# First two column blocks of a mixer's output projection multiplied together, three of eight ktile pairs by seven products of block sums

## The chip, the core and the metric

The kernel runs on one core of one Trainium2 chip. Its engines work side by side and in order: TensorE (in the profile PE, its weight loads PEld), VectorE (DVE), ScalarE (ACT), GpSimd (POOL) and SyncE (SP); SP and POOL also have queues from which transfers are issued. The time is the device time of one execution in microseconds; a run's value is compared as the median over executions, lower is better.

## What is computed

One layer of a decoder trunk on 256 tokens of width 2048. The part that matters is the mixer's end and what follows it:

```python
merged = g[:, :, 0] * (o_a @ w_o_mla) + g[:, :, 1] * (o_b @ w_o_swa)   # (256, 2048)
y = merged @ w_out                                                      # w_out: (2048, 2048)
x = x + rms_norm(y, norm_mix_post)
h = rms_norm(x, norm_ffn_pre)
x = x + rms_norm(conv_ffn(h, w_up, conv_w, conv_b, w_down), norm_ffn_post)
```

All arrays are float32.

## The kernel before

**Products.** A float32 operand is split into a high part that TensorE's fp32r form takes and the low rest. `mm3` (line 174) makes one product of three matmuls, high by high, high by low, low by high, each with a 128x128 block of activations as the stationary operand and 128x512 weights as the moving one. Weights come as raw tiles of 128x1024 float32 through a ring of three buffers (`raw_row`, `wchunk`; transfers on SP's queue). `convert` (line 134) makes the parts: a cast on ScalarE (line 143), the difference on VectorE (line 144). The results go into a ring of converted chunks, five deep in this part of the kernel (`RING` = 4 and one more from `flex[0] = "w"`, line 896). A chunk's buffer is free again when its matmuls are done.

**A projection.** `gemm` (line 179) makes one block of 512 output columns for both tiles of 128 tokens: 16 ktiles (128 rows of weights each), two ktiles a chunk, 16 x 2 x 3 = 96 matmuls into two PSUM banks. After each chunk it calls `tick`, which runs the work that `at` has put at that step; this is how work of one stage is written out between the matmuls of another. `drain` runs what is left. A scheduler then fixes each engine's order ahead of time; an engine doesn't change it at run time.

**The stages around the change.** `wo_a` is multiplied in four blocks (lines 835 to 843). After each, VectorE joins the two branches (lines 840 and 841), and in the next block's steps `m_cols` transposes the merged activations on TensorE and splits them (lines 820, 233, 234) into `mt`, eight tiles of two ktiles each. During the first of these blocks the gain `gpost` and the residual `x2` are loaded on SP's queue (`late_loads`, lines 804 to 810). Then `w_out` is multiplied in four blocks of 512 columns (lines 898 to 913). After each, `y_evac` squares it on ScalarE for the norm (line 857) and multiplies it by the gain on VectorE into `yg` (line 858). Block 3 finishes its first token tile ahead of the second; `resid` (line 865) then adds the normed result to `x2`, and the FFN begins.

**PSUM.** There are eight banks: four in `pacc`, two in `pss`, two in `pst`. All `gemm` calls of `wo_a` and `w_out` take two of `pacc`; the transposes of `m_cols` take `pst`.

**Seven products.** The FFN's down projection, later in the kernel, already has the other form. `down_pair` (line 1096) takes two column blocks and 12 ktile pairs. A ktile pair by two column blocks and two token tiles is a 2 by 2 product of blocks. A plain step (`p`) makes its eight block products, 24 matmuls. A seven step (`s`) makes seven, 21 matmuls, from sums of activation blocks (`token_sums`, line 1017, made once in an earlier stage) and differences of weight blocks (lines 1131 to 1134, on VectorE), with the Winograd form of Strassen's scheme. The results go to four banks `c` and four banks `q`; the latter are added together after the last seven (lines 1148 to 1152). The raw weights of a seven are loaded on POOL's queue (lines 1126, 1127). `PAIR_ORDER` (line 1240) gives the steps of the two pairs, `psppsppsppsp` and `ppsppsppsppp`.

Of the kernel before, what the change touches and what calls it, by code (L numbers as in the profile page):

```python
# [19 lines left out]
P = 128  # L20
D = 2048
# [20 lines left out]
def trunk_layer(ctx, tc, x, x_cols_in, conv_cols_in, g_mix_post, g_ffn_post, w_in, w_q, w_kv,  # L42
# [136 lines left out]
    def gemm(xh, xl, w, k0, nk, c0, n, split=None, extra=None, ps=None):  # L179
# [19 lines left out]
        return acc, todo  # L199

# [598 lines left out]
    x2_all = [sb(p3, [P, D], f"x2_{t}") for t in range(NT)]  # L799
    x2 = [[x_[:, j * 512:(j + 1) * 512] for j in range(4)] for x_ in x2_all]  # L800
    es6, p6 = open_pool("p6")
    gpost = sb(p6, [P, D], "gpost", tag="gp")
# [30 lines left out]
    for i in range(12):  # L833
        at(now[0] + 10 + 2 * i, lambda i=i: late_loads(i))
    for j in range(4):
        ld = merge_loads(j)
        acc, _ = gemm(AH, AL, wo_a, 0, KT, 512 * j, 512)
# [8 lines left out]
    yg_all = [[sb(p6, [P, 1024], f"yg_{t}_{j}", tag="f" + "ab"[t], bufs=2) for j in range(2)] for t in range(NT)]  # L846
    yg = [[yg_all[t][j // 2][:, (j % 2) * 512:(j % 2 + 1) * 512] for j in range(4)] for t in range(NT)]
# [6 lines left out]
    def y_evac(acc, b, t):  # L854
# [3 lines left out]
        vec.tensor_tensor(yg[t][j][:, o:o + n], acc[t][:, :n], gpost[:, c0:c0 + n], op=ALU.mult)  # L858
# [36 lines left out]

    flex[0] = "w"
    turn.update(raw=0, w=0)
    for b in range(4):
        c0, n = W_BLOCKS[b]
        last = b == 3  # L900
        acc, todo = gemm(MH_, ML_, w_out, 0, KT, c0, n, split=0 if last else None, extra={i: (px,) for i in range(EXTRA)} if last else None)
        if b == 0:
            drain()
            es4.close()
            es8, p8 = open_pool("p8")
# [111 lines left out]
    def token_sums(u):  # L1017
# [4 lines left out]
        g = gtiles[u].bitcast(F32)  # L1022
        a, m = (sb(s_pool[0], [P, 512], f"s{n}{u}", tag="hx", bufs=2) for n in "am")
        vec.tensor_tensor(a, g[:, 0:512], g[:, 512:1024], op=ALU.add)
        a11, a21, a12, _ = (a[:, i * P:(i + 1) * P] for i in range(4))
        m1, m2, m3, m4 = (m[:, i * P:(i + 1) * P] for i in range(4))
        vec.tensor_tensor(m1, a21, a[:, 384:512], op=ALU.add)
        vec.tensor_tensor(m3, a11, a21, op=ALU.subtract)
        vec.tensor_tensor(m2, m1, a11, op=ALU.subtract)
# [285 lines left out]
```

## Time and profile before

| | us |
|---|---|
| median of 3 runs (1471.06 to 1471.63) | 1471.11 |
| the profiled execution | 1471.75 |
| its span, from the first to the last instruction | 1470.0 |
| DVE busy in the span | 1023.2 |
| ACT busy in the span | 818.1 |

The page names each group of instructions by line of the kernel, engine, operation, and tile written and tiles read. "DVE wlo L144 <- ACT whi L143" in a list of waits says that VectorE's instruction of line 144 had to wait for ScalarE's of line 143; the numbers are total us, times and longest. Times within the execution count from the start of the span. In this count `wo_a`'s last block begins near 621 and `w_out` at 643.6; the down projection's two pairs run from 1004.5 to 1130.3. Some matmul records are missing from the trace.

### The profile page before, as it was taken

The numbers are of one execution on the slowest core, as the hardware profiler recorded it, in microseconds if no ns is written. First come the engines' busy times: TensorE is split into PE (matmuls) and PEld (weight loads), VectorE is DVE, ScalarE is ACT, GpSimd is POOL, SyncE is SP. The second block draws the span as 40 slices with busy tenths as digits, with TensorE's granted clock in tenths as the row PEclk, the third lists the DMA queues.
The fourth block names the chain that finished last, engine by engine and source line by source line (L and its number), as shares of the span: only waits on it lengthen the run. The fifth ranks groups of instructions, "written<-read, shape, count | busy, mean of one in ns | idle before, by whom it ended". The sixth has DMA issues, their size and how long they took to land.

```text
span 1470.0 us, 20862 instructions
## 1 busy us (share of the span) xinstructions
PE 1460.2 (99%) x7594; PEld 1247.9 (85%) x7594; DVE 1023.2 (70%) x1793; ACT 818.1 (56%) x1352; POOL 58.6 (4%) x101
## 2 busy tenths in 40 slices
PE   9999999999999999999999999999999999999997
PEld 7888888888888888888888888888888888888886
DVE  7788884445667665555699976778786676677556
ACT  7588864443555554444566655555454555555443
POOL 0022100000000000000000000000000000000000
PEclk9999999999999999999999999999999999999999
DMA  8755376666655549656766666665657666666663
GB/s 301 211 173 166 95 215 192 208 207 201 193 156 160 161 163 337 225 192 203 225 202 185 196 189 188 188 188 188 223 174 261 200 185 196 189 186 189 197 189 127
DMA packets 154513, 287.58 MB, mean 196 GB/s; under 512 B 18427, under 2 KB 29596, under 8 KB 154284
## 3 DMA queue, kind: packets, MB, share of 16 engines
q1 hardware_dynamic: 147648, 263.09, 58.0%
q0 software_dynamic: 6672, 23.12, 5.0%
q8 instruction: 59, 0.97, 0.3%
q14 instruction: 42, 0.34, 0.1%
q10 hardware_dynamic: 92, 0.05, 0.0%
HBM read 277.79 MB, written 8.44 MB: 195 GB/s over the span
## 4 chain that ended last, share of the span: by engine, by line
PE 96%; DVE 2%; ACT 1%; issue 1%; DVEq 0%
PE accg L175 15%; PE accg L177 15%; PE accg L176 15%; PE ub L1041 10%; PE ua L1041 10%; PE ub L1045 5%; PE ua L1045 5%; PE c L176 2%; PE c L175 2%; PE c L177 2%; PE mpo L760 1%; PE ms L726 1%; PE qn L689 1%; PE qn L691 1%; PE qn L690 1%
## 5 line engine op out<-in xcount | busy, mean ns | idle before, releaser
L144 DVE TENSOR_TENSOR wlo<-raw,whi 128x1024 fp32r<-128x1024 f32 (+2 forms) x488 | 591.9, 1216 | 347.2 <-ACT whi L143 342.4
L143 ACT CAST whi<-raw 128x1024 fp32r<-128x1024 f32 (+2 forms) x488 | 507.9, 1043 | 469.8 <-PE accg L177 246.3
L175 PE MATMUL accg<-whi,ahl 128*128 128x512 f32 (+1 forms) x544 | 212.8, 391 | 0.0
L177 PE MATMUL accg<-whi,ahl 128*128 128x512 f32 (+1 forms) x544 | 210.4, 387 | 0.0
L176 PE MATMUL accg<-wlo,ahl 128*128 128x512 f32 (+1 forms) x544 | 209.6, 385 | 0.0
L175 PE MATMUL accg<-whi,bhl 128*128 128x512 f32 x442 | 173.1, 392 | 0.0
L177 PE MATMUL accg<-whi,bhl 128*128 128x512 f32 x442 | 172.3, 390 | 0.0
L176 PE MATMUL accg<-wlo,bhl 128*128 128x512 f32 x442 | 172.2, 390 | 0.0
L1041 PE MATMUL ua<-ahl,whi 128*128 128x512 f32 x640 | 154.6, 391 | 0.0
L1041 PE MATMUL ub<-ahl,whi 128*128 128x512 f32 x640 | 154.6, 391 | 0.0
L1041 PEld LDWEIGHTS ub<-ahl,whi 128*128 128x128 f32 x640 | 117.5, 188 | 22.9 <-ACT cc L930 0.2
L1041 PEld LDWEIGHTS ua<-ahl,whi 128*128 128x128 f32 x640 | 117.5, 188 | 22.7
L177 PEld LDWEIGHTS accg<-whi,ahl 128*128 128x128 f32 x544 | 102.1, 188 | 20.5
L176 PEld LDWEIGHTS accg<-wlo,ahl 128*128 128x128 f32 x544 | 102.3, 188 | 18.1
L175 PEld LDWEIGHTS accg<-whi,ahl 128*128 128x128 f32 x544 | 102.2, 188 | 17.7
L177 PEld LDWEIGHTS accg<-whi,bhl 128*128 128x128 f32 x442 | 83.0, 188 | 17.3
L176 PEld LDWEIGHTS accg<-wlo,bhl 128*128 128x128 f32 x442 | 83.0, 188 | 17.0
L175 PEld LDWEIGHTS accg<-whi,bhl 128*128 128x128 f32 x442 | 83.0, 188 | 16.8
L1045 PEld LDWEIGHTS ub<-ahl,wlo 128*128 128x128 f32 x640 | 82.2, 191 | 3.2
L1045 PEld LDWEIGHTS ua<-ahl,wlo 128*128 128x128 f32 x640 | 82.2, 191 | 3.1
L1045 PE MATMUL ua<-ahl,wlo 128*128 128x256 f32 x640 | 83.7, 283 | 0.0
L1045 PE MATMUL ub<-ahl,wlo 128*128 128x256 f32 x640 | 83.2, 283 | 0.0
(433 smaller groups left out, 1905.4 us busy)
## 6 DMA issues: line engine op xcount, KB each, us to landing
raw<-in_ffn_w_up_dram SPq DMA_DIRECT2D x176, 512.0 KB, 4.4
raw<-in_w_in_dram SPq DMA_DIRECT2D x111, 512.0 KB, 4.5
raw<-in_ffn_w_down_dram SPq DMA_DIRECT2D x74, 512.0 KB, 3.9
raw<-in_w_o_swa_dram SPq DMA_DIRECT2D x32, 512.0 KB, 4.3
raw<-in_w_o_mla_dram SPq DMA_DIRECT2D x32, 512.0 KB, 4.7
raw<-in_w_out_dram SPq DMA_DIRECT2D x32, 512.0 KB, 4.1
bias<-strip POOLq DMA_DIRECT2D x16, 256.0 KB, 4.3
raw<-in_mla_w_q_up_dram SPq DMA_DIRECT2D x32, 128.0 KB, 2.5
```

Source lines behind the costliest of these rows:

```text
L143: act.copy(hi[:, a:b], raw[:, a:b])
L144: vec.tensor_tensor(lo[:, a:b], raw[:, a:b], hi[:, a:b].bitcast(F32), op=ALU.subtract)
L175: pe.matmul(o, ah, bh, start=start, stop=False)
L176: pe.matmul(o, ah, bl, start=False, stop=False)
L177: pe.matmul(o, al, bh, start=False, stop=stop)
L689: pe.matmul(o, wh, ch(k), start=k == 0, stop=False)
L690: pe.matmul(o, wh, cl(k), start=False, stop=False)
L691: pe.matmul(o, wl, ch(k), start=False, stop=k == nk - 1)
L726: pe.matmul(o, w, v_, start=n == 0, stop=False)
L760: pe.matmul(o, w(t), p_[:, c], start=n == 0, stop=n == 5)
L1041: pe.matmul(acc[i], hi[:, c], hn[p][:, j * 512:(j + 1) * 512], start=p + j == 0, stop=stop)
L1045: pe.matmul(acc[i][:, 0:256], lo[:, c], hn[p][:, j * 512:j * 512 + 256], start=False, stop=False)
```

## The change

`down_pair` becomes a general `pair_gemm`, which the down projection calls as before, now with its four `c` additions behind it. `w_out`'s column blocks 0 and 1 are made by it together, with `W_ORDER = "ppspspsp"`: ktile pairs 0, 1 and 2 by seven products, pairs 3 to 7 plain. Blocks 2 and 3 stay as they were. For this:

- `m_sums` makes the token sums of pairs 0 to 2 during `wo_a`'s blocks 2 and 3, into `ms`, which takes the place where `x2` will be; `x2` is loaded during block 2 of `w_out` instead.
- The first and third seven's raw weights take buffers of `px`, the second's the buffer of `gpost`; `gpost` is loaded after that, on POOL's queue.
- The weights' differences take the buffers of `yg` for blocks 2 and 3; the sum of `q` takes those of blocks 0 and 1.
- `wo_a`'s block 3 and `w_out`'s block 2 use the `pss` banks. The last two `m_cols` come one step earlier.
- Squares and gain products of blocks 0 and 1 are made from `yg` after `c` is added to it.

```diff
+    def pair_gemm(name, w, k0, c0, order, act_of, s_of, kind, d, place, sums):
+
+        c11, c12, c21, c22 = c = banks(kind, f"c{name}_")
+        q, used = [], set()
+        row = lambda k: w[(k0 + k) * P:(k0 + k + 1) * P, c0:c0 + 1024]
...
+        def plain(u, last):
+            for k in (2 * u, 2 * u + 1):
+                w_ = convert(raw_row(row(k)), 1024)
+                for t in range(NT):
+                    for j in range(2):
+                        mul(c[2 * t + j], act_of(k, t), half(w_, j), last and k % 2 == 1)
+                tick()
+
+        def seven(u, last):
+            s1, s2, s3, s4 = s_of(u)
+            even, odd = place()
+            pool.dma_start(even, row(2 * u))
+            pool.dma_start(odd, row(2 * u + 1))
+            ta, tb = sums()
+            lo_, hi_ = slice(0, 512), slice(512, 1024)
+            w_ = convert(odd, 1024)
+            vec.tensor_tensor(ta[:, lo_], even[:, hi_], even[:, lo_], op=ALU.subtract)
+            vec.tensor_tensor(ta[:, hi_], odd[:, hi_], even[:, hi_], op=ALU.subtract)
+            vec.tensor_tensor(tb[:, lo_], odd[:, hi_], ta[:, lo_], op=ALU.subtract)
+            vec.tensor_tensor(tb[:, hi_], odd[:, lo_], tb[:, lo_], op=ALU.subtract)
+            if not q:
+                q[:] = banks(1 - kind, f"q{name}_")
+            q1, q5, q7, q6 = q
+            mul(c11, act_of(2 * u + 1, 0), half(w_, 0))
+            mul(c12, s4, half(w_, 1))
+            w_ = convert(even, 512)
+            mul(q1, act_of(2 * u, 0), half(w_, 0), last)
+            w_ = convert(ta, 1024)
+            mul(q5, s1, half(w_, 0), last)
+            mul(q7, s3, half(w_, 1), last)
+            tick()
+            w_ = convert(tb, 1024)
+            mul(q6, s2, half(w_, 0), last)
+            mul(c21, act_of(2 * u + 1, 1), half(w_, 1))
+            tick()
+            if last:
+                act.copy(d[0], q1)
+                vec.tensor_tensor(d[1], d[0], q6, op=ALU.add)
+                vec.tensor_tensor(d[2], d[1], q7, op=ALU.add)
+                vec.tensor_tensor(d[3], d[2], q5, op=ALU.add)
+                vec.tensor_tensor(d[1], d[1], q5, op=ALU.add)
...
+    def token_sums(g, a, m, hi, lo):
+
+        vec.tensor_tensor(a, g[:, 0:512], g[:, 512:1024], op=ALU.add)
+        a11, a21, a12, a22 = (a[:, i * P:(i + 1) * P] for i in range(4))
+        m1, m2, m3, m4 = (m[:, i * P:(i + 1) * P] for i in range(4))
+        vec.tensor_tensor(m1, a21, a22, op=ALU.add)
+        vec.tensor_tensor(m3, a11, a21, op=ALU.subtract)
+        vec.tensor_tensor(m2, m1, a11, op=ALU.subtract)
+        vec.tensor_tensor(m4, a12, m2, op=ALU.subtract)
+        split_to(hi, lo, m)
...
-            nc.sync.dma_start(gpost[:, i * 512:(i + 1) * 512], g_mix_post[i * 512:(i + 1) * 512].partition_broadcast(P))
+            if i == 0:
+                gpost.append(sb(p6, [P, D], "gpost", tag="gp"))
+            pool.dma_start(gpost[0][:, i * 512:(i + 1) * 512], g_mix_post[i * 512:(i + 1) * 512].partition_broadcast(P))
...
-    for i in range(12):
-        at(now[0] + 10 + 2 * i, lambda i=i: late_loads(i))
...
+        if j == 2:
+            for u in range(W_ORDER.count("s")):
+                at(now[0] + 2 + 4 * u, lambda u=u: m_sums(u))
+        acc, _ = gemm(AH, AL, wo_a, 0, KT, 512 * j, 512, ps=(pss, "s") if j == 3 else None)
...
-            at(now[0] + (3 if j == 3 else 1) + p, lambda p=2 * j + p, ld=ld: m_cols(p, ld))
+            at(now[0] + (2 if j == 3 else 1) + p, lambda p=2 * j + p, ld=ld: m_cols(p, ld))
...
+    def w_place():
+        w_done[0] += 1
+        i = w_done[0]
+        if i % 2:
+            return [sb(px, [P, 1024], f"mr{i}{n}", tag="w" + n) for n in ("hi", "lo")]
+        both = sb(p6, [P, D], f"mr{i}", tag="gp")
+        at(now[0] + 2, *(lambda k=k: late_loads(k) for k in range(4)))
+        return both[:, 0:1024], both[:, 1024:2048]
+
+    def w_pair():
+        d = [yg[t][j] for t in range(NT) for j in range(2)]
+        c = pair_gemm("w", w_out, 0, 0, W_ORDER, lambda k, t: (MH_(k)[:, t * P:(t + 1) * P], ML_(k)[:, t * P:(t + 1) * P]),
+                      lambda u: ms[u], 0, d, w_place, lambda: [yg_all[t][1] for t in range(NT)])
+        for i, (o, x_) in enumerate(zip(d, c)):
+            vec.tensor_tensor(o, o, x_, op=ALU.add)
+        for i, o in enumerate(d):
+            t, j = divmod(i, 2)
+            act.activation(jk(f"yj{j}_{t}"), o, AF.Square, accum_out=ssy[t][:, j:j + 1])
+            vec.tensor_tensor(o, o, gpost[0][:, j * 512:(j + 1) * 512], op=ALU.mult)
+
     flex[0] = "w"
     turn.update(raw=0, w=0)
-    for b in range(4):
+    w_pair()
+    drain()
...
+    for i in range(4, 12):
+        at(now[0] + i - 4, lambda i=i: late_loads(i))
+    for b in range(2, 4):
...
+W_ORDER = "ppspspsp"
```

More of the change, by code (lines that the diff above doesn't have):

```diff
@@ new lines, in token_sums @@
+    def token_sums(g, a, m, hi, lo):
[7 more added lines that the diff above has]
+        split_to(hi, lo, m)
+        return [[x[:, i * P:(i + 1) * P] for x in (hi, lo)] for i in range(4)]
@@ L1015, in trunk_layer, with g_sums @@
     s_tiles = []
-    def token_sums(u):
+    def g_sums(u):
         if u % 2 == 0:
@@ L1081, in trunk_layer @@
             for u in range(4):
-                at(now[0] + 3 + 3 * u, lambda u=u: token_sums(u))
+                at(now[0] + 3 + 3 * u, lambda u=u: g_sums(u))
         ffn_up(c, 4 * c)
```

136 lines of the change are left out of this document (47 added, 89 removed).

## The prediction

> **What bounds the kernel now.** I read the page's head and chain first, then the list of waits for PE alone, then stretches and the order of time around the two places that matter: `w_out`'s first two column blocks, and the FFN's down projection, where this kernel already multiplies by seven products.
>
> ```profile
> span 1470.0 us, 20862 instructions
> PE 1460.2 (99%) x7594; PEld 1247.9 (85%) x7594; DVE 1023.2 (70%) x1793; ACT 818.1 (56%) x1352; POOL 58.6 (4%) x101
> PE 96%; DVE 2%; ACT 1%; issue 1%; DVEq 0%
> ```
> ```profile
> PE warm L77 <- DVE ramp L66: 1.1, 1, 1.1
> ```
>
> TensorE (PE) is busy 99% of the span and the chain that ends last lies 96% on it. The second fence is all that the list of waits has for PE: one wait, 1.1 us, at the start. So nothing is late for PE anywhere near the change: a matmul taken away shortens the kernel by its slot, and anything that makes PE wait lengthens it. What a slot costs must be read with care, because the records of matmuls overlap. In order of time, `w_out`'s first matmul, then the down projection's first pair, its first matmul and its end:
>
> ```profile
> 643.61 0.39 PE L175 MATMUL accg<-whi,ahl 128*128 128x512 f32 x1
> ...
> 1004.49 0.39 PE L175 MATMUL c<-whi,bhl 128*128 128x512 f32 x1
> ...
> 1056.85 0.39 PE L175 MATMUL c<-whi,bhl 128*128 128x512 f32 x1
> 1057.07 0.39 PE L176 MATMUL c<-wlo,bhl 128*128 128x512 f32 x1
> ...
> 1061.61 0.39 PE L175 MATMUL c<-whi,ghl 128*128 128x512 f32 x1
> ...
> 1067.05 0.39 PE L175 MATMUL c<-whi,bhl 128*128 128x512 f32 x1
> ```
>
> A record lasts 0.39 us, but the next matmul starts after 0.22; the last row is the second pair's first. From 1056.85 to 1061.61 runs one step by seven products (21 matmuls), from there to 1067.05 one plain step (24): 4.76 and 5.44 us, and 4.76/21 = 5.44/24 = 0.2267 us. That is the price of a slot, and the two intervals are the old and new price of one ktile pair.
>
> **What is removed.** In the two blocks, eight ktile pairs at 2 ktiles x 2 token tiles x 2 blocks x 3 matmuls = 24 are 192 slots, 43.5 us. Three pairs fall to 21: 9 slots, 3 x 0.68 = **2.04 us less**. Blocks 2 and 3 keep their 96 matmuls each, and the transposes of the merged activations stay eight per column block. So PE's own work in the pair is 5 x 5.44 + 3 x 4.76 = 41.5 us.
>
> **What is added, mostly on VectorE (DVE).** The rows for its price, then the stretches that show what PE tolerates:
>
> ```profile
> L144 DVE TENSOR_TENSOR wlo<-raw,whi x488: 687/1225/1580, 4.8 to 1449.4; 128x1024 fp32r<-128x1024 f32 x158, 128x640 fp32r<-128x640 f32 x3, 128x512 fp32r<-128x512 f32 x2
> L1133 DVE TENSOR_TENSOR tb<-rr,ta x4: 686/686/689, 1002.6 to 1089.5; 128x512 f32<-128x512 f32 x4
> L1149 DVE TENSOR_TENSOR ds<-ds,q x2: 680/680/680, 1062.1 to 1114.2; 128x512 f32<-128x512 f32 x2
> L840 DVE SCALAR_TENSOR_TENSOR lta<-lta,accg x8: 681/682/684, 575.1 to 643.9; 128x512 f32<-128x512 f32 x8
> L234 DVE SCALAR_TENSOR_TENSOR ahl<-mT,ahl x8: 682/684/685, 583.3 to 660.1; 128x512 fp32r<-128x512 f32 x8
> L143 ACT CAST whi<-raw x488: 614/1053/1111, 4.2 to 1448.4; 128x1024 fp32r<-128x1024 f32 x158, 128x640 fp32r<-128x640 f32 x3, 128x512 fp32r<-128x512 f32 x2
> ```
> ```profile
> 597.90:643.61 45.71, 45.71 (x210) 37.78 (x209) 26.87 (x30) 19.79 (x21) 3.75 (x7) 1.00 0.63 204
> 643.61:686.90 43.29, 43.29 (x196) 35.84 (x195) 24.44 (x25) 19.11 (x22) 0.00 (x0) 1.00 0.64 212
> 1004.49:1025.57 21.08, 21.08 (x95) 17.45 (x93) 19.91 (x33) 12.15 (x19) 2.12 (x4) 1.00 0.54 180
> 1025.57:1061.61 36.04, 36.04 (x161) 29.84 (x159) 27.67 (x29) 19.03 (x20) 2.64 (x5) 1.00 0.64 208
> ```
>
> In the first fence the three numbers are the shortest, median and longest instruction in ns; in the second each row gives a stretch, its length, then busy time of PE, PEld, DVE, ACT and POOL, then PE's granted clock (1.00 throughout), DMA share and GB/s.
>
> A plain ktile row is converted once: 1.05 us on ACT, then 1.22 on DVE. A seven needs three full conversions, one of half width (0.69) and four differences of weights (0.69 each): 3.67 + 0.69 + 2.75 = 7.1 us of DVE for 4.76 of PE. DVE's work over the pair, then: ten rows 12.2; three sevens 21.3; the last merge block's four operations 2.7; two activation splits (L234) 1.4; the four additions that empty the seven's banks 2.7. Together **40.4 us in 41.5**, where the stretch now holds 24.4 in 43.3. ACT stays easy: 19 casts at 1.05 and 3 at 0.61 are 21.8 us. The four additions onto the accumulators, four squares and four gain products (5.5 us of DVE) come after the pair, beside block 2, where DVE has 1.5 us to spare in each 2.72 us chunk.
>
> Whether 97% hurts is the whole question, and the down projection answers it in part. Over 1004.49 to 1025.57 (plain, seven, plain, plain) DVE was busy 19.91 of 21.08 us, 94%, and PE lost nothing: four seven-product and eight plain steps should take 62.6 us, and the pair ran 62.56, from 1004.49 to 1067.05. But there a seven comes once in three steps; the new order, two plain and then seven and plain in turn three times, has one in two: 9.5 us of DVE in each 10.2 of PE.
>
> I placed DVE's work by hand against the ring of five converted chunks: a chunk's cast may begin when PE releases the fifth before it. With each instruction as soon as it can go, the tightest chunk, the first plain row behind a seven, is ready about 1.5 us before its use (released at the seven's start, then 1.05 + 1.22 and a queue of up to 1 us, against 4.76). So no stall if DVE's order is as good as that; what a poor order costs is the slower rival below. I take **zero**, nearest the 94% stretch; the bounds are 0 (PE has nothing else to shed there) and 8.5 us, the slower rival's.
>
> The first seven's differences need no matmul; part of them can run in the last merge block, where DVE idles. So do the three token sums: each is two 512-wide operations and four of 128 columns, an estimated 2.5 us from the 0.69 row and a quarter of it plus a start, 7.5 in all; the stretch 597.90 to 643.61 alone has 45.7 - 26.9 = 18.8 us free.
>
> **PSUM.** Block 3 of the merge moves to the pss banks, which the sevens' q1 and q5 and then block 2 use. The price at its end is shown by the down projection, where the next pair takes the same banks:
>
> ```profile
> 1059.37 0.57 ACT L1148 COPY ds<-q 128x512 f32<-128x512 f32 x1
> 1062.07 0.68 DVE L1149 TENSOR_TENSOR ds<-ds,q 128x512 f32<-128x512 f32 x1
> 1064.11 0.68 DVE L1152 TENSOR_TENSOR ds<-ds,q 128x512 f32<-128x512 f32 x1
> ```
>
> The last addition ended at 1064.79 and the next pair began at 1067.05: 2.3 us to spare, and block 2 touches q5's bank only three slots (0.68 us) in. If DVE first converts two chunks more (2.4 us) it still fits; at three it costs 0.7. I take zero. The transposes of the last merged columns move one chunk earlier; the seven's q7 and q6 wait for their banks, 12 slots (2.7 us) behind, against 0.6 + 0.7 us of evacuation: zero.
>
> **Transfers.** Six weight loads of 512 KB and the four gain loads go to POOL's queue, eight loads of x move on SP's from the merge to block 2. Prices:
>
> ```profile
> L1126 POOL DMA_DIRECT2D rr<-in_ffn_w_down_dram x4: 528/535/542, 739.2 to 1073.0; - x4
> DMA to landing us min/median/max: 3.7/5.4/6.5
> 630.32 0.54 POOL L828 DMA_DIRECT2D lta<-ta_d  x1 [6.41 <-PE mT L820]
> gpost<-in_norm_mix_post_dram SPq DMA_DIRECT2D x4, 256.0 KB, 5.9
> x<-in_x_dram SPq DMA_DIRECT2D x8, 256.0 KB, 7.0
> L872 DVE SCALAR_TENSOR_TENSOR x<-yg,ry_y,x x8: 743/744/750, 726.3 to 744.5; 128x512 f32<-128x512 f32 x8
> ```
>
> POOL's queue is free from 630.9, 12.7 us before the pair, so the first two sevens' weights land long before use. The gain loads wait until the second seven's sums have been read (about 21 us into the pair), and the third seven's loads stand behind them in program order. Issued in that order: 21 + 4 x 0.54 + 2 x 0.54 + 5.4 = 29.6 us, plus conversion 2.3 = 31.9, against a use at 31.3. That would cost about 0.6 us at the first chunk and, with four differences following, some 2. But the third seven's buffers are free from the start, and the same queue took the down projection's first loads at 739.2, 265 us ahead of that pair: I take zero, bound 2.0. The x loads queue between raw rows on SP; 8 chunks of block 2 end near 643.6 + 41.5 + 21.8 + 1 = 708 and the last lands by 715, before 726.3.
>
> **The sum.** The profiled execution took 1471.75 us (span 1470.0 and 1.75 around it), 0.64 over the median. 1471.75 - 2.04 + 0 = 1469.71; from the median, 1471.11 - 2.04 = **1469.1 us**. That is 0.14% less. About 0.2%, 2.9 us, is what a measurement of this kernel can tell from no change, so the forecast is "within".
>
> **The rivals.**
>
> *VectorE becomes the bound (slower).* Place: the three sevens. In 1025.57 to 1061.61 DVE idled 8.4 of 36.0 us, 23%, mostly waiting for a cast that waited for a ring slot; the list of waits over the down pairs (985 to 1135) says so:
>
> ```profile
> DVE wlo L144 <- ACT whi L143: 28.5, 30, 2.4
> ACT whi L143 <- PE c L177: 30.7, 24, 2.1
> ```
>
> If that share is forced by the instruction order, 40.4 us of work need 52.5, against 41.5 + 2.5 that the ring gives ahead (4.76 - 2.27): PE waits about 8.5 us, and the time is 1477.6. It decides from 8% forced idle on, eats the gain at 12%, and is slower by over 0.2% from 18%. For it: one seven in every two steps. Against: 6% idle in the 94% stretch, so the idle shrinks when there is work. 17%.
>
> *Small waits.* A late bank or late third loads: 0.5 to 5 us, typically 2, so 1471.1. For it: three margins of 1.5 to 2.3 us. Against: no such wait in the pair of the same form. 14%.
>
> *Loads on POOL's queue stretched while VectorE is busy (slower).* If each third load took twice the longest seen, 13 us in place of 5.4, the 2 us of that bound become 9.6 and the time 1478.7; slower by over 0.2% from 8.4 us a load on. Against: DVE was 77 to 94% busy while the down projection's loads took 3.7 to 6.5. 1%.
>
> [...]
>
> *A matmul is worth its record.* 9 x 0.39 = 3.5 us and 1467.6, if taking out products frees more than slots. For it: only the grouped means. Against: the 4.76 and 5.44. 10%.
>
> *The forecast*, no new wait of 0.5 us: 58%.
>
> **The numbers.** Faster by over 0.2% is the fourth rival, 0.10; slower the first and third, 0.18; within is the rest, 0.72. The range runs from 1467.5, which takes in the 1467.6, to 1476.0, which leaves out the upper half of the first rival and the third: about 3 in a hundred lie below and 10 above, the rest is allowance for what no row shows. The likeliest case's own range is 1468.7 to 1469.6.
>
> **What would show it.** Right: PE's list of waits stays empty around the pair; seven-product steps start 4.76 us and plain ones 5.44 apart; the two blocks take 41.5 us and the transposes; DVE is near 97% there. Wrong: a wait of PE's weight loads or matmuls on `wlo` (VectorE), on a copy or addition out of q (banks), or gaps before a seven while its load is under way. A saving above 2.5 us would mean that slots are not the price.

## The result, and the profile after

Compared on one chip, the changed kernel's median is 1474.58 us (1473.27 to 1477.33) and that of the kernel before 1471.15 (1470.27 to 1472.16): ratio 1.0022, 95% interval [1.0016, 1.0028]. The change makes the kernel slower by about 3 us where 2 us less were forecast. The profiled execution took 1475.55 us. From its page, the head, the engines and the chain that ended last:

```profile
span 1473.7 us, 20893 instructions
PE 1460.5 (99%) x7585; PEld 1246.0 (85%) x7585; DVE 1046.2 (71%) x1837; ACT 824.5 (56%) x1362; POOL 63.8 (4%) x111
PE 93%; DMA 3%; DVE 2%; ACT 1%; issue 1%; DVEq 0%; SPq 0%; ACTq 0%
```

PE lost 9 matmul records, as it should (7594 to 7585). But 3% of the chain is now DMA, which had no part in it before. The list of waits for PE alone had one line before; after, it has four:

```profile
PE accg L176 <- DVE wlo L144: 2.7, 4, 0.9
PE warm L77 <- DVE ramp L66: 1.1, 1, 1.1
PE x2T L962 <- DVE x L959: 0.3, 1, 0.3
PE pstrip L341 <- DMA sel<-in_strip_sel_dram: 0.3, 1, 0.3
```

`accg` at line 176 is `gemm`, not the pair (whose banks are called `cw`). So PE waits for converted weights in blocks 2 and 3, behind the pair that was changed. PE in order of time: the pair's first matmul, block 2's first, then two places where a matmul started late:

```profile
644.48 0.39 PE L175 MATMUL cw<-whi,ahl 128*128 128x512 f32 x1
...
686.93 0.39 PE L175 MATMUL accg<-whi,ahl 128*128 128x512 f32 x1
...
692.37 0.39 PE L175 MATMUL accg<-whi,ahl 128*128 128x512 f32 x1
693.66 0.50 PE L176 MATMUL accg<-wlo,ahl 128*128 128x512 f32 x1 [0.90 <-DVE wlo L144]
...
719.38 0.50 PE L175 MATMUL accg<-whi,ahl 128*128 128x512 f32 x1
720.64 0.50 PE L176 MATMUL accg<-wlo,ahl 128*128 128x512 f32 x1 [0.76 <-DVE wlo L144]
```

The pair took 686.93 - 644.48 = 42.45 us: 41.5 of products and some 1 us of transposes, 2.04 less than the 44.49 of the same part before. The loss stands behind it. 693.66 - 692.37 is 1.29 us where a slot is 0.2267, so 1.06 us are lost at the third chunk of block 2; the rest is lost in block 3's first pass, which multiplies one token tile only, but for 0.45 us at the first `x2` transpose behind it (0.25 before).

I therefore cut each trace at four points: the first matmul of `w_out`, block 2's first, the first transpose of `x2`, and the first matmul of w_up's main loop (`ua`, line 1146; the expectations below call it the first of w_up). "Waits" is the sum over the matmuls from block 2's start to the first `x2` transpose of what their starts are apart beyond a slot. The list above counts a wait only from the end of the record before, so its 0.90 is 1.06 here; "waits" also takes in matmuls that run slowly, which matters in e5. All in us, from PE's order of time:

| | pair | block 2 to `x2` transpose | to `ua` | whole stage | waits |
|---|---|---|---|---|---|
| before | 44.49 | 39.02 | 52.85 | 136.35 | 0.25 |
| after | 42.45 | 43.54 | 52.74 | 138.74 | 4.56 |

-2.04 + (4.56 - 0.25) = +2.27, of the stage's 2.39. The rest of the 3.7 us by which the two spans differ lies outside: 0.87 ahead of `w_out`, whose start lies anywhere from 642.65 to 644.48 in the traces of this study, and 0.43 behind. So the stage is the sharper measure, and the tables below give it beside the ratio.

What is late shows in VectorE's order of time. Before, and then after, around block 2's start (688.10 and 686.93):

```profile
678.51 1.23 DVE L144 TENSOR_TENSOR wlo<-raw,whi 128x1024 fp32r<-128x1024 f32 x1 [1.49 <-ACT whi L143]
681.23 1.22 DVE L144 TENSOR_TENSOR wlo<-raw,whi 128x1024 fp32r<-128x1024 f32 x1 [1.49 <-ACT whi L143]
683.73 1.23 DVE L144 TENSOR_TENSOR wlo<-raw,whi 128x1024 fp32r<-128x1024 f32 x1 [1.27 <-ACT whi L143]
686.67 1.23 DVE L144 TENSOR_TENSOR wlo<-raw,whi 128x1024 fp32r<-128x1024 f32 x1 [1.72 <-ACT whi L143]
```
```profile
680.81 1.23 DVE L144 TENSOR_TENSOR wlo<-raw,whi 128x1024 fp32r<-128x1024 f32 x1 [0.21 <-ACT whi L143]
681.95 0.68 DVE L253 TENSOR_TENSOR yg<-yg,qw 128x512 f32<-128x512 f32 x1
...
684.59 1.22 DVE L144 TENSOR_TENSOR wlo<-raw,whi 128x1024 fp32r<-128x1024 f32 x1
685.73 2.48 DVE L999 TENSOR_TENSOR yg<-yg,cw 128x512 f32<-128x512 f32 x4
689.51 2.96 DVE L1003 TENSOR_TENSOR yg<-yg,gpost 128x512 f32<-128x512 f32 x4 [1.31 <-ACT yj L1002]
692.39 3.49 DVE L144 TENSOR_TENSOR wlo<-raw,whi 128x1024 fp32r<-128x1024 f32 x3
698.54 1.22 DVE L144 TENSOR_TENSOR wlo<-raw,whi 128x1024 fp32r<-128x1024 f32 x1 [2.66 <-ACT whi L143]
```

Before, the four conversions shown are block 2's first four chunks, 10.9 us of PE's work ready when it begins. After, only two are ready (680.81 and 684.59), and then VectorE converts nothing from 685.8 to 692.4: the four additions, 1.31 us of idling for the squares, and the four gain products stand ahead in its queue. ScalarE and SyncE at the same place:

```profile
682.99 1.05 ACT L143 CAST whi<-raw 128x1024 fp32r<-128x1024 f32 x1 [2.22 <-DMA raw<-in_w_out_dram]
686.49 1.05 ACT L143 CAST whi<-raw 128x1024 fp32r<-128x1024 f32 x1 [2.44 <-PE cw L177]
687.81 1.05 ACT L143 CAST whi<-raw 128x1024 fp32r<-128x1024 f32 x1 [0.27 <-DMA raw<-in_w_out_dram]
688.76 0.63 ACT L1002 ACTIVATE yj<-yg 128x512 f32<-128x512 f32 x1
...
691.65 1.03 ACT L143 CAST whi<-raw 128x1024 fp32r<-128x1024 f32 x1
697.45 1.05 ACT L143 CAST whi<-raw 128x1024 fp32r<-128x1024 f32 x1 [4.76 <-DMA raw<-in_w_out_dram]
```
```profile
685.84 0.38 SPq L131 DMA_DIRECT2D raw<-in_w_out_dram  x1
686.26 0.47 SPq L891 DMA_DIRECT2D x<-in_x_dram  x1
693.67 6.49 SPq L131 DMA_DIRECT2D raw<-in_w_out_dram  x4
```

The casts of block 2's third and fourth chunk (686.49 and 687.81) were done by 688.9, but their differences come 4 to 5 us later. A load buffer is free only then, so SyncE issues no weights from 686.2 to 693.7, and ScalarE waits 4.76 us for a load at 697. The hole in one queue runs through all three. In the lists of waits from 686 to the first transpose, before and then after, the cause of the casts' idle time changes over:

```profile
ACT whi L143 <- DMA raw<-in_w_out_dram: 8.4, 7, 1.8
ACT whi L143 <- PE accg L177: 5.5, 5, 1.9
```
```profile
ACT whi L143 <- DMA raw<-in_w_out_dram: 16.3, 11, 4.8
ACT whi L143 <- PE accg L177: 0.7, 1, 0.7
```

A cast that waits for PE has found all places for converted chunks full: a reserve. After, it waits for loads instead: the reserve is gone.

### The profile page after: what moved, and what is told of

The parts are those of the page before. It is cut to its first block, busy times and chain, and to the rows that moved or that the text cites. A ratio compares the mean times of both kernels' runs of the same rounds, so it can differ in the third digit from the quotient of the medians.

```text
span 1473.7 us, 20893 instructions
## 1 busy us (share of the span) xinstructions
PE 1460.5 (99%) x7585; PEld 1246.0 (85%) x7585; DVE 1046.2 (71%) x1837; ACT 824.5 (56%) x1362; POOL 63.8 (4%) x111
## 4 chain that ended last, share of the span: by engine, by line
PE 93%; DMA 3%; DVE 2%; ACT 1%; issue 1%; DVEq 0%; SPq 0%; ACTq 0%
PE accg L175 13%; PE accg L177 13%; PE accg L176 13%; PE ub L1146 10%; PE ua L1146 10%; PE ub L1150 5%; PE ua L1150 5%; PE cd L177 2%; PE cd L176 2%; PE cd L175 2%; DMA raw<-in_w_out_dram 2%; DVE wlo L144 1%; PE mpo L839 1%; DMA raw<-in_w_in_dram 1%; PE ms L805 1%
## 5 line engine op out<-in xcount | busy, mean ns | idle before, releaser
L144 DVE TENSOR_TENSOR wlo<-raw,whi 128x1024 fp32r<-128x1024 f32 (+2 forms) x482 | 583.8, 1215 | 325.6 <-ACT whi L143 318.2
L143 ACT CAST whi<-raw 128x1024 fp32r<-128x1024 f32 (+2 forms) x482 | 501.2, 1043 | 464.0 <-PE accg L177 223.9
L176 PE MATMUL accg<-wlo,ahl 128*128 128x512 f32 (+1 forms) x480 | 185.3, 386 | 2.7 <-DVE wlo L144 2.7
L175 PE MATMUL accg<-whi,ahl 128*128 128x512 f32 (+1 forms) x480 | 187.9, 392 | 0.0
L177 PE MATMUL accg<-whi,ahl 128*128 128x512 f32 (+1 forms) x480 | 185.6, 387 | 0.0
L176 PEld LDWEIGHTS accg<-wlo,ahl 128*128 128x128 f32 x480 | 90.2, 188 | 20.0 <-DVE wlo L144 4.5
L177 PEld LDWEIGHTS accg<-whi,ahl 128*128 128x128 f32 x480 | 90.1, 188 | 17.9
L175 PEld LDWEIGHTS accg<-whi,ahl 128*128 128x128 f32 x480 | 90.2, 188 | 15.9 <-ACT whi L143 0.5
```

Of the source, the lines that this page charges most:

```text
L143: act.copy(hi[:, a:b], raw[:, a:b])
L144: vec.tensor_tensor(lo[:, a:b], raw[:, a:b], hi[:, a:b].bitcast(F32), op=ALU.subtract)
L175: pe.matmul(o, ah, bh, start=start, stop=False)
L176: pe.matmul(o, ah, bl, start=False, stop=False)
L177: pe.matmul(o, al, bh, start=False, stop=stop)
```

## The experiments

The theories at the start: **A**, the run of additions, squares and products behind the pair holds up the conversions. **B**, the loads of x between the weight loads on SyncE's queue do it (**B2**: they do the rest once A is mended). **C**, VectorE's load inside the pair is too high as such. **D**, with the last seven so near the pair's end, the three load buffers are held by rows that wait behind it. Later came **E**: block 3's first pass needs a reserve of converted chunks that the pair's end doesn't leave. Each kernel was run eleven times (e9 five) beside the kernel before on the same chip.

**e1_spread.** The squares and products one by one, in four steps of block 2; the additions stay.

```diff
-        for i, o in enumerate(d):
-            t, j = divmod(i, 2)
-            act.activation(jk(f"yj{j}_{t}"), o, AF.Square, accum_out=ssy[t][:, j:j + 1])
-            vec.tensor_tensor(o, o, gpost[0][:, j * 512:(j + 1) * 512], op=ALU.mult)
+    for i in range(4):
+        at(now[0] + 2 + i, lambda i=i: w_evac(i))
```

> The change with one thing moved: the four squares and four gain products of blocks 0 and 1 no longer stand together right behind the pair, but one tile's at a time behind chunks 2 to 5 of block 2. Theory A (the evacuation stands in VectorE's and ScalarE's queues ahead of block 2's conversions, the lead in converted chunks is lost, and block 3's fast first pass runs it out): the conversions of block 2 wait no more than about 1 us, the 4.5 us of waits in blocks 2 and 3 go, and the time is 1471.1 - 2.0 = 1469 us, 1469 to 1470. Rival B (the loads of x, moved into block 2, delay the raw weights): no change, 1474 to 1475. Rival C (the sevens overload VectorE): no change, 1474 to 1475.

**e2_no_x_loads.** The loads of x are replaced by zeroes made on GpSimd.

```diff
-            nc.sync.dma_start(x2[t][j], x[t * P:(t + 1) * P, j * 512:(j + 1) * 512])
+            pool.memset(x2[t][j], 0.0)
```

> The change with the eight loads of x left out and x set to zero by GpSimd in their place (the residual of this half is left out), all else the same. Rival B: raw weights land in time, 1469 to 1470 us. Theory A: VectorE's order is the same and so are the waits in block 2; at most some of those in block 3 shrink, as raw weights land a little sooner: 1473 to 1475.

**e3_all_plain.** No sevens, the rest of the new form kept: copies stand where the additions were, and the gain is loaded at the pair's start.

```diff
-W_ORDER = "ppspspsp"
+W_ORDER = "pppppppp"
...
-            vec.tensor_tensor(o, o, x_, op=ALU.add)
+            vec.tensor_copy(o, x_)
```

> The change with W_ORDER of eight plain pairs: no seven products, no sums of weights, nine matmuls more; the accumulators of blocks 0 and 1 are copied where the additions were, and squares and products stand behind the pair as in the change. The gain is loaded at the pair's start. Rival C: no overload, so the time of before, 1471 us. Theory A: the run of copies, squares and products is still there, so block 2 and 3 still wait, about as much as in the change or somewhat less (one conversion stands between the copies): 1473 to 1476.

| | pair | block 2 to `x2` transpose | whole stage | waits | ratio |
|---|---|---|---|---|---|
| e1_spread | 42.45 | 40.84 | 136.05 | 2.02 | 1.0000 [0.9991, 1.0009] |
| e2_no_x_loads | 42.45 | 44.07 | 139.30 | 5.03 | 1.0023 [1.0014, 1.0032] |
| e3_all_plain | 44.49 | 39.01 | 136.31 | 0.25 | 1.0000 [0.9991, 1.0009] |

B falls: without the x loads nothing is better. A is half right: spreading takes 2.5 us of waits away, and the wait at the start of block 2 is gone; 2.0 us stay, nearly all in block 3's first pass and at the `x2` transpose. And A is not enough by itself: e3 has such a run too, and PE doesn't feel it. VectorE in e3:

```profile
682.76 1.23 DVE L144 TENSOR_TENSOR wlo<-raw,whi 128x1024 fp32r<-128x1024 f32 x1 [1.27 <-ACT whi L143]
...
685.91 1.22 DVE L144 TENSOR_TENSOR wlo<-raw,whi 128x1024 fp32r<-128x1024 f32 x1
687.04 1.88 DVE L1001 COPY yg<-cw 128x512 f32<-128x512 f32 x3
688.84 2.49 DVE L1005 TENSOR_TENSOR yg<-yg,gpost 128x512 f32<-128x512 f32 x4
691.24 2.36 DVE L144 TENSOR_TENSOR wlo<-raw,whi 128x1024 fp32r<-128x1024 f32 x2
```

The run, 687.04 to 691.3, is 4.3 us in place of 6.6. What is more, 685.91 is block 2's fourth conversion (its start is 687.14), so four chunks are ready as in the kernel before. The run costs nothing when there is a reserve to live on.

**e4_spread_no_x**, **e5_order**, **e6_spread_order**, **e7_spread_raw.** e4 is e1 with e2's edit. e5 is the changed kernel with the second and third seven each moved one step forward, e6 the same on e1. e7 is e1 with block 2's first weights loaded outside the three buffers:

```diff
-W_ORDER = "ppspspsp"
+W_ORDER = "ppsspspp"
```
```diff
-        acc, todo = gemm(MH_, ML_, w_out, 0, KT, c0, n, split=0 if last else None, extra={i: (px,) for i in range(EXTRA)} if last else None,
+        acc, todo = gemm(MH_, ML_, w_out, 0, KT, c0, n, split=0 if last else None, extra={i: (px,) for i in range(EXTRA)} if last else {0: (None, p8)},
```

> The spread version (squares and products one tile at a time in block 2) and also without the loads of x, set to zero by GpSimd in their place (the residual of this half is left out). Theory B2 (once the evacuation is spread, the x loads are what keeps block 3 waiting 1.9 us): the waits in block 3 go, 2.0 us under the kernel before. Theory D (while the last seven's four short chunks pass through the ring of converted chunks, the last plain rows sit unconverted in the three raw buffers, so block 2's first loads are issued about 5 us later against PE than before, and three buffers do not catch up): waits of at least 1 us stay, 1 us under before at most.

> The change with W_ORDER ppsspspp in place of ppspspsp: the same products, but four plain rows stand behind the last seven in place of two; the evacuation stands in one run behind the pair as in the change. Theory D: block 2's loads are issued earlier against PE, so the lead is fuller when the run of evacuation comes, as it is in the all-plain version: the 4.5 us of waits shrink to 1.5 or less, 0 to 2 us under before. Theory A alone (the run of evacuation is the cost): no change, 3 us over before. Theory C: two sevens in a row are 14.2 us of VectorE in 9.5 of PE, so PE waits inside the pair and the time is higher than the change's.

> Spread evacuation and W_ORDER ppsspspp together. Theory D with A: no wait of PE in the pair, block 2 or block 3 beyond those of before, 2.0 us under before (ratio 0.9986). Theory C: waits in the pair, over before.

> Spread evacuation with the order of the change, and the raw weights of block 2's first chunk in a buffer of their own, so that its load waits for no raw buffer. Theory D: the loads of block 2 run one buffer earlier, the 1.9 us of waits shrink by about a chunk's supply, to under 1 us: 1 to 2 us under before. Theory B2: no change from the spread version, equal to before.

| | pair | block 2 to `x2` transpose | whole stage | waits | ratio |
|---|---|---|---|---|---|
| e4_spread_no_x | 42.45 | 41.01 | 136.27 | 2.18 | 0.9997 [0.9988, 1.0006] |
| e5_order | 42.45 | 43.27 | 138.43 | 4.47 | 1.0001 [0.9992, 1.0011] |
| e6_spread_order | 42.45 | 40.80 | 136.02 | 1.97 | 0.9995 [0.9986, 1.0004] |
| e7_spread_raw | 42.45 | 42.89 | 138.13 | 4.04 | 1.0006 [0.9997, 1.0015] |

B2 falls (2.2 us of waits without any x load). C falls, though e3 came out at the time that C gave: e5 and e6 set two sevens side by side and their pair still takes 42.45. D is not borne out with the spreading: e6 has e1's waits. e5 has to be read with care. Of its 4.47 us, some 1.6 are matmuls that ran at half clock (granted 0.50 from 721 to 724, see the last section), so its waits as such are 2.9, none of them at the start of block 2. The profiled execution was the slowest of eleven (1474.43 of 1470.92 to 1474.43) and the one with the lowest granted clock (0.997; the others 0.998 or 0.999), so most of the others probably kept their full clock. By its median e5 lies 0.4 us over the kernel before, where e2, which keeps the change's order, lies 3.3 over it on the same chip: the order alone regains most of the loss. VectorE's order of time in e5 shows the third conversion ahead of the additions (685.91) and the fourth between the gain products (690.05), so the new order broke up the run as well; whether that or D's load buffers did it, e5 doesn't part. e7 was a miss: three chunks were ready when block 2 began, but the scheduler set a gain product ahead of the next conversions, VectorE idled 2.5 us for its square, and the waits doubled.

What is left in e1 is where theory E came from. VectorE in e1, in block 2:

```profile
692.12 1.23 DVE L144 TENSOR_TENSOR wlo<-raw,whi 128x1024 fp32r<-128x1024 f32 x1 [0.99 <-ACT whi L143]
...
699.15 1.23 DVE L144 TENSOR_TENSOR wlo<-raw,whi 128x1024 fp32r<-128x1024 f32 x1 [1.50 <-ACT whi L143]
```

With two conversions between them these are three chunks in 7.03 us, 2.34 each: each conversion waits for its cast, the cast for its load, the load for one of three buffers. Block 2 uses a chunk in 12 slots, 2.72 us, so its reserve grows by 0.38 a chunk. Block 3's first pass uses one in 6 slots, 1.36 us, and its reserve shrinks by 0.98 a chunk, 7.8 us over eight.

**e8_split2**, **e9_after_split2**, **e10_fewer.** e8 (on e6) and e9 (on the changed kernel) let the first two chunks of block 3 multiply both token tiles at once. `carry` lets the second tile's bank go on accumulating when its other chunks follow. e10 is the kernel before with nine matmuls of block 1 left out (`mm2` is `mm3` without its last product).

```diff
-        acc, todo = gemm(MH_, ML_, w_out, 0, KT, c0, n, split=0 if last else None, extra={i: (px,) for i in range(EXTRA)} if last else None,
+        acc, todo = gemm(MH_, ML_, w_out, 0, KT, c0, n, split=2 if last else None, carry=last, extra={i: (px,) for i in range(EXTRA)} if last else None,
...
-            finish_tile(acc[1], todo)
+            finish_tile(acc[1], todo, carry=True)
```
```diff
-                        mm3(acc[t][:, :n], *x_, wh, wl, kt == 0,
+                        (mm2 if t and 0 < kt <= fewer else mm3)(acc[t][:, :n], *x_, wh, wl, kt == 0,
...
-        acc, todo = gemm(MH_, ML_, w_out, 0, KT, c0, n, split=0 if last else None, extra={i: (px,) for i in range(EXTRA)} if last else None)
+        acc, todo = gemm(MH_, ML_, w_out, 0, KT, c0, n, split=0 if last else None, extra={i: (px,) for i in range(EXTRA)} if last else None, fewer=9 if b == 1 else 0)
```

> Additions, squares and gain products spread, order ppsspspp, and the first two chunks of block 3 multiplied by both halves of the tokens at once (a chunk then lasts 2.72 us of TensorE instead of 1.36), the other six by the second half afterwards as before. Theory E: a load buffer comes round every 7.06 us (issue to the end of its conversion), three of them give a chunk each 2.35 us, and the first pass of block 3 uses one each 1.36 us, so it lives on the chunks converted ahead; behind the pair that lead is short by about 2 us, and so the 2.0 us of waits. Two chunks at the slower pace give 2.72 us: waits in blocks 2 and 3 fall from 2.0 to under 0.7 us, the stage from the first matmul of w_out to the first of w_up is 134.0 to 135.0 us instead of 136.0, the time 1.0 to 2.0 us under before (ratio 0.9986 to 0.9993). Rival: the waits come from the evacuation's place in the queues (A) and not from the pace of block 3; then it stays at 136.0 us and ratio 0.9995 to 1.0005.

> The changed kernel with nothing else than the first two chunks of block 3 multiplied by both halves of the tokens at once. Theory E: of its 4.5 us of waits the 1.06 us at the start of block 2 stays (there it is the run of additions, squares and products itself), the waits in block 3's first pass, 3.0 us, fall by up to 2.72: stage 136.0 to 136.8 us instead of 138.7, ratio 1.0000 to 1.0008. Rival A alone (the run of additions, squares and products is the whole cause): nothing moves, 138.5 us and ratio 1.0018 to 1.0028.

> The kernel before, with nine matmuls of block 1 left out (the product of the low part of the activations, second half of the tokens, k tiles 1 to 9: the output misses these small terms). 2.04 us less of TensorE in the same stage and nothing else changed. Theory E: the ring of converted chunks is full when block 2 starts, so the gain stays: stage 134.3 to 134.6 us instead of 136.35, ratio 0.9984 to 0.9988. Rival F (the stage's length is set by the supply of chunks from its start on, and any time saved ahead of block 3 is waited for there; the first transposes of x2 came 83.25 to 83.5 us after the first matmul of w_out in five of eight kernels): stage 136.0 to 136.4 us, 2 us of waits in block 3's first pass, ratio 0.9998 to 1.0002.

| | pair | block 2 to `x2` transpose | whole stage | waits | ratio |
|---|---|---|---|---|---|
| e8_split2 | 42.45 | 45.05 | 139.11 | 3.57 | 1.0021 [1.0012, 1.0030] |
| e9_after_split2 | 42.45 | 49.38 | 143.29 | 7.76 | 1.0052 [1.0039, 1.0064] |
| e10_fewer | 44.49 | 36.98 | 134.27 | 0.26 | 0.9985 [0.9976, 0.9994] |

("Block 2" begins 44.49 us in for e10 too, so that its missing slots show in the second column.) e10 came out as E had it: 2.04 us less of PE with full reserves is 2.08 less of the stage, so rival F, a floor under the stage, falls. And a slot is worth 0.2267 us. e8 and e9 missed their numbers. In e8 no wait was left in block 3's first pass, but one of 3.57 us had come where it ends, at the first `x2` transpose. VectorE and PE in e8:

```profile
721.57 1.23 DVE L144 TENSOR_TENSOR wlo<-raw,whi 128x1024 fp32r<-128x1024 f32 x1 [1.23 <-ACT whi L143]
724.20 1.23 DVE L144 TENSOR_TENSOR wlo<-raw,whi 128x1024 fp32r<-128x1024 f32 x1 [1.41 <-ACT whi L143]
725.35 0.15 DVE L955 TENSOR_REDUCE vy<-ssy 128x1 f32<-128x4 f32 x1
```
```profile
726.91 0.39 PE L177 MATMUL accg<-whi,ahl 128*128 128x512 f32 x1
730.71 1.32 PE L962 MATMUL x2T<-ident,x 128*128 128x128 f32 x8 [3.41 <-DVE x L959]
...
732.45 0.63 PE L177 MATMUL accg<-whi,ahl 128*128 128x512 f32 x1
732.88 0.63 PE L175 MATMUL accg<-whi,ahl 128*128 128x512 f32 x1
```

The two early chunks gave their places outside the ring back early. The scheduler used these for chunks of w_up, and three conversions of w_up that still waited for loads stood ahead of the residual's reduction (L955), which PE's transposes need. It is A's mechanism again at another place: an instruction that nobody needs yet waits for a load, and one that is needed stands behind it. e9 shows the same wait, 4.9 us long.

**e11_split2_late_px**, **e12_after_late_px.** As e8 and e9, but the places outside the ring go to the third to fifth chunk.

```diff
-        acc, todo = gemm(MH_, ML_, w_out, 0, KT, c0, n, split=2 if last else None, carry=last, extra={i: (px,) for i in range(EXTRA)} if last else None,
+        acc, todo = gemm(MH_, ML_, w_out, 0, KT, c0, n, split=2 if last else None, carry=last, extra={i + 2: (px,) for i in range(EXTRA)} if last else None,
```

> As e8_split2, but the three converted chunks of block 3 that lie outside the ring are its third to fifth instead of its first to third. In e8 the waits of block 3's first pass were gone and a wait of 3.57 us at the first transpose of x2 had come: the first two chunks gave their places back early, so three conversions of w_up stood ahead of the residual's operations in VectorE's queue, each behind a load; now they give back ring places and one conversion of w_up stands there, as in the kernel before. Theory E with this reading: no wait over 0.5 us in blocks 2 and 3, stage 134.0 to 134.7 us (before 136.35), ratio 0.9982 to 0.9990. Rival: the slower pace only moves the shortage from block 3's chunks to those of w_up, whose loads share the three buffers; then waits of 1.5 to 2 us stand at x2's transposes or in the first product of w_up, stage 135.6 to 136.4 us, ratio 0.9995 to 1.0003.

> The changed kernel, its additions, squares and gain products still in one run and its order unchanged, with the split after two chunks and the later places of e11 alone. It parts the 4.5 us of waits. Theory E plus A: the 1.0 us at the start of block 2 stays, because the run of additions, squares and products makes it before any of block 3 is used; of the 3.0 us in block 3's first pass up to 2.72 go: waits 1.0 to 1.8 us, stage 135.3 to 136.0 us, ratio 0.9992 to 1.0002. If the run of additions, squares and products were the whole cause: 4 us of waits, 138 us and more, ratio over 1.0010.

e11: waits 0.20, stage 136.27, ratio 0.9998 [0.9989, 1.0007]. e12: waits 3.23, stage 138.95, ratio 1.0016 [1.0007, 1.0025]. The reserve was mended in e11, yet the stage was not shorter. PE now waited past the `x2` transposes:

```profile
PE accg L175 <- ACT bhl L966: 1.2, 1, 1.2
...
PE accg L177 <- DVE bhl L969: 0.4, 1, 0.4
```

`bhl` is w_up's activation, scaled from the transposes. ScalarE's order shows what stood ahead of it:

```profile
737.56 0.62 ACT L974 ACTIVATE xj<-x 128x512 f32<-128x512 f32 x1
...
740.45 2.15 ACT L966 ACTIVATE bhl<-x2T,gmat 128x128 fp32r<-128x128 f32 x8
```

Four squares for the next norm, 2.9 us, whose sum is used only at the end of that product. So e11's time is the rival's, but the shortage had not moved to w_up's chunks, as the rival had it. e12 kept its 1.0 us at block 2 as expected, but also 1.4 us in block 3, and its stage is the one that its expectation gave to A alone (138 us and more). I read it as a reserve that behind the unspread run is short by more than two slow chunks give; no further run tests that.

**e13_split2_queue**, **e14_split1_queue**, **e15_before_split2.** e13 is e11 with the squares issued behind those scalings; like e11 it has the squares and products of e1 spread and e5's order. e14 has one slow chunk in place of two. e15 puts those edits of e13 that lie behind the first two blocks (slow chunks, later places, squares) into the kernel before.

```diff
-            act.activation(jk(f"xj{t}_{j}"), x2[t][j], AF.Square, accum_out=ssh[t][:, j:j + 1])
+            with tc.issue_after(bh_last[0].ins):
+                act.activation(jk(f"xj{t}_{j}"), x2[t][j], AF.Square, accum_out=ssh[t][:, j:j + 1])
```
```diff
-        acc, todo = gemm(MH_, ML_, w_out, 0, KT, c0, n, split=2 if last else None, carry=last, extra={i + 2: (px,) for i in range(EXTRA)} if last else None,
+        acc, todo = gemm(MH_, ML_, w_out, 0, KT, c0, n, split=1 if last else None, carry=last, extra={i + 1: (px,) for i in range(EXTRA)} if last else None,
```

> As e11_split2_late_px, and the eight squares of x2 (ScalarE, for the norm ahead of w_up) are issued behind the scalings of x2's transposes into the activations of w_up instead of ahead of them. In e11 the first pass of block 3 had no wait left (0.2 us in blocks 2 and 3), and 1.2 and 0.4 us stood at the first matmuls of w_up that read the second half of the tokens: four squares, 2.9 us, had gone ahead of the scalings in ScalarE's queue. Theory E plus queue order: with both out of the way the saved 2.04 us shows: stage 134.2 to 134.9 us (before 136.35, e11 136.27), ratio 0.9982 to 0.9992. Rival G (a chain of work on VectorE, ScalarE and the loads sets the end of the stage, so a wait removed at one place comes back at the next): stage 135.8 to 136.4 us and ratio 0.9995 to 1.0005.

> As e13 with one chunk of block 3 at the slower pace instead of two, and the places outside the ring from its second chunk on. It gives block 3's first pass 1.36 us instead of 2.72. Theory E: of the 2.0 us of waits that e6 had, 0.4 to 0.8 stay; stage 134.7 to 135.2 us, ratio 0.9986 to 0.9996. Rival G: 135.8 to 136.4 us, ratio 0.9995 to 1.0005.

> The kernel before with e13's three edits behind the first two blocks alone (two chunks of block 3 at the slower pace, later places outside the ring, squares of x2 behind the scalings). Theory E: its ring is full when block 2 starts and it has 0.25 us of waits to lose there, so nothing moves: stage 136.0 to 136.4 us, ratio 0.9997 to 1.0003. If these edits are a gain of their own, ratio under 0.9993: then what e13 gains is not the change's.

| | pair | block 2 to `x2` transpose | to `ua` | whole stage | waits | ratio |
|---|---|---|---|---|---|---|
| e13_split2_queue | 42.45 | 41.69 | 50.96 | 135.10 | 0.21 | 0.9992 [0.9983, 1.0001] |
| e14_split1_queue | 42.45 | 40.33 | 55.51 | 138.29 | 0.21 | 1.0021 [1.0013, 1.0030] |
| e15_before_split2 | 44.49 | 41.74 | 51.04 | 137.27 | 0.26 | 1.0008 [1.0000, 1.0017] |

e13 against e15 is the change with its run spread and its sevens moved forward, the queues behind it mended in both: 135.10 against 137.27, 2.17 us less, and medians of 1470.72 and 1473.16, 2.4 less. The 2.04 us are there once nothing behind the pair is late; rival G falls, though e13 lies 0.2 us over its own forecast of 134.2 to 134.9. The mending has a price of its own, 0.9 us of stage in e15, where nothing was expected: two chunks' matmuls fewer lie behind the transposes to cover `bhl`, and PE loses 0.8 us there. So of 2.04 us e13 keeps 1.25 over the kernel before, and its interval still touches 1. It is the quickest kernel of the study that leaves nothing out. e14 missed: block 3's first pass was free of waits with one slow chunk, but a cast of w_up now stood ahead of the scalings, behind a load, and PE lost 1.7 us at one matmul, and more at half clock behind it (granted 0.51 from 743 to 746):

```profile
740.06 1.04 ACT L143 CAST whi<-raw 128x1024 fp32r<-128x1024 f32 x1 [4.20 <-DMA raw<-in_ffn_w_up_dram]
741.01 1.13 ACT L968 ACTIVATE bhl<-x2T,gmat 128x128 fp32r<-128x128 f32 x4
```

Over the fifteen runs, the stage's distance from 136.35 and the median's from the kernel before on the same chip agree within 0.65 us except for e5 and e7 (1.7 and 1.0); in e5 the difference is about what the profiled execution lost at half clock. For the changed kernel itself they differ by 1.0 us, 2.39 against 3.43; that part stays unexplained.

## Why the prediction was wrong

**What held.** PE bounded the kernel, and a slot is 0.2267 us: the pair is 2.04 us shorter in every trace that has the sevens, and e10 shows what such slots are worth when nothing else moves. The step put down at zero for VectorE inside the pair was right: no matmul of the pair waits, in e5 and e6 not even with two sevens in a row. The wait on `wlo` that was to show an error did come, but behind the pair. PSUM and the loads on GpSimd's queue cost nothing that a trace shows; the x loads fall with e2 and e4. The third rival's 13 us for a load, and its part in the 0.18 for slower, rest on no run: the sevens' six weight loads took 7.0 to 11.0 us, at 44% busy VectorE and a DMA share of 1.02 (552.4 to 575.0 of the changed kernel), and none was read before 585.5. The first rival, VectorE as the bound inside the sevens, named the wrong place, and a matmul was not worth its record. That 1474.58 lies inside the range of 1467.5 to 1476.0 is luck: its upper part was made for waits inside the pair, and none came there.

**The step that failed** is "The four additions onto the accumulators, four squares and four gain products (5.5 us of DVE) come after the pair, beside block 2, where DVE has 1.5 us to spare in each 2.72 us chunk", costed at nothing. The sum over engines is right, the order is not: the additions and products, with the idle time for the squares, held VectorE for 6.6 us in one piece, ahead of the conversions that PE and the load buffers waited for. Spreading the squares and products takes 2.5 of the 4.3 us of new waits away (e1). The prediction asked inside the pair what a poor order costs; behind the pair it didn't ask what is queued behind these operations and who waits for that.

**What the prediction left out** is the reserve. It asked whether any chunk in the pair comes late, not how many are ready when the pair ends: two in place of four, where by the estimate above block 3's first pass draws 7.8 us on the reserve. I put the 2.0 us that stay in e1 down to it; that two slow chunks in block 3 leave 0.20 (e11) bears this out. VectorE was less full in the pair than I worked out, 35.6 us busy (84%) in place of 40.4 (97%): the first seven's four differences ran long before it, and part of the rest is block 2's chunks that were not yet converted. At the pair's end VectorE was not what came late: ScalarE's cast of block 2's second chunk had waited 2.22 us for its load (682.99), that of the third 2.44 us for PE to free a place (686.49). So the load buffers, and the ring's places (a seven puts four pieces into it where a plain pair of ktiles puts two), are the likelier reasons why the reserve is short. That is read from one trace; which share is theirs and which VectorE's, no run here parts.

**The rival on small waits** gave a size, 0.5 to 5 us, that takes in the 4.6 that came, but put the waits at banks and third loads, where there are none. That too is luck.

## What to carry to other kernels

When an operation is put behind a stage, give it a place in each in-order queue and write down what stands behind it there and how long that can wait; free time summed over a stage says nothing of one piece of 6.6 us. A stage that uses its inputs faster than they are made lives on what the stages ahead of it have stored, so a change that fills a helper engine must be checked at the next fast stage, not only where it is made. And in a schedule fixed ahead of time, each mending shifts other instructions: look for the needed one that stands behind one that waits for a load.

## What the hardware showed unexpectedly

In some of the runs PE was slow for a while behind its waits. In e8 the 3.57 us wait was followed by matmuls 0.427 us apart (732.45, 732.88 above) in place of 0.2267. The stretches of e8 (start and end, length, busy time of PE, PEld, DVE, ACT and POOL, granted clock, DMA share, GB/s) show the clock:

```profile
732.40:735.50 3.10, 3.10 (x9) 2.37 (x8) 2.67 (x7) 2.11 (x6) 0.96 (x2) 0.50 0.97 363
735.50:740.00 4.50, 4.50 (x25) 3.76 (x24) 3.14 (x16) 4.10 (x13) 1.07 (x2) 0.99 0.30 97
```

The granted clock was 0.50 for about 3 us, so seven slots of that time cost 0.2 us each: some 1.4 us on top of the wait. In e8 the wait on PE thus cost some 40% more than its length. e5 shows the same behind waits of 1.2 and 1.0 us close together (granted 0.50 from 721 to 724; in the 3 us ahead PE was busy for 1.17), and e14 behind waits of 1.7 and 0.6 (0.51 from 743 to 746; in the 3 us ahead PE was busy for 1.15). e9, with a wait of 4.9 us, had a mean granted clock of 0.997 in each of its executions, where the kernel before had 0.998 or 0.999 beside it. The changed kernel, whose three waits of some 1 us lie 2.5 us and more apart, kept its full clock (1.00 in every 5 us from 690 to 735). So did e7 with waits of 0.8, 1.0, 0.6 and 1.0 us within 5.4 us (0.999 over the execution), more in sum than those of e5 and e14, so how much idling it takes is not settled here.
